# Three of the first layer's last four modulation chunks on VectorE, beside the input projection

## The chip, the cores and the metric

The kernel runs on one core of a Trainium2 chip. The metric is the device time of one execution in microseconds. A run of the program is timed as a whole; one execution is also profiled, and the profile gives the start and the duration of every instruction on every engine. In what follows the engines are called as the profile calls them: PE is TensorE (matmuls; PEld its weight loads), DVE is VectorE, ACT is ScalarE, POOL is GpSimd, and SP issues most DMAs.

## The reference

One inference step of a two-layer backbone, on 512 latent tokens and 128 context tokens of width 1024. What the change touches is the modulation, six vectors per layer and condition (shift, scale and gate of the mixer, then of the FFN):

```python
def modulation(cvec, w_mod, b_mod):
    m = jax.nn.silu(cvec) @ w_mod + b_mod
    return jnp.split(m[:, None, :], 6, axis=-1)

def run_trunk(x, cvec, p, past):
    ...
    for i in range(DEPTH):
        j = i // 2
        sh1, sc1, g1, sh2, sc2, g2 = modulation(cvec, p['w_mod'][i], p['b_mod'][i])
        h = rmsnorm(x, p['norm_mix'][i]) * (1.0 + sc1) + sh1
        if i % 2 == 0:
            ...
            mix, s_fin = even_mixer(h, p, j, s0)
        ...
        x = x + g1 * (mix @ p['w_out'][i])
        h = rmsnorm(x, p['norm_ffn'][i]) * (1.0 + sc2) + sh2
        x = x + g2 * conv_ffn(h, p['ffn_w_up'][i], p['ffn_conv_w'][i], p['ffn_conv_b'][i], p['ffn_w_down'][i])
```

There are two conditions: the vector c for the latent tokens and the constant c_ctx for the context tokens. A weight `w_mod[i]` is 1024 x 6144. The first layer's mixer (`even_mixer`) projects h to 3600 columns, runs four heads of a gated DeltaNet in both directions over chunks of tokens, and an implicit long convolution of order two (Hyena) on the other 512 columns.

## The kernel before, in words

Activations lie transposed, 128 features by 642 columns (512 latent tokens, a gap of two, 128 context tokens). A product with a weight is made of three matmuls with operands split in a high and a low part (lines 310 to 312); for that every weight tile `wr` is copied to `wwh` by ACT (line 304) and the rest taken to `wwl` by DVE (line 305).

Modulations come in chunks of 1024 columns, so six per layer, numbered as in the reference: 0 and 1 are needed before the first layer's projection, 2 (g1) by its output projection, 3 and 4 (shift and scale) by its FFN's norm, 5 (g2) at the end of its FFN. They are computed in one of two ways:

- `mod_chunk` on PE: eight steps over the 1024 rows. Each loads a 128 x 1024 piece of `w_mod` into a buffer `wr` and issues four matmuls with the two conditions as stationary operand (32 columns wide, four strips of the array) into one PSUM bank `modps`. `mod_finish` then copies the bank to SBUF (`mev`, ACT), transposes it twice on PE (`modt`) and adds the bias on DVE.
- `mod_rows` on DVE: the two conditions are loaded as rows spread over all partitions (`crow`) and put through SiLU on ACT; the weight comes transposed in pieces `mraw`; each piece of 128 x 512 is multiplied with the row of each condition and summed along the row by one instruction (line 257, output `mjunk`, sums in `mpart`). A chunk has 8 x 2 pieces and two conditions, so 32 such instructions, and two small additions at its end. All of layer 1's chunks are done in this way.

Chunks 0 and 1 of layer 0 run on PE in the prologue, among the filters of the Hyena part (`filters`). Then the input projection starts: `heads_in` and `hyena_in` call `unit_T`, a projection unit of 128 columns (a weight load, the split, 48 matmuls; its matmul results are called `mm`, the convolved result `cv`). `fills` yields, in this order, the second half of the heads, all Hyena units and the gates (`dn_gate`, `zT`); after these it sets `ready[0]`, and then comes the Hyena transform (`hyena_order`: matmuls `fx`, `iv`, `ivp`, with `rab`, `yab`, `hy` on the other engines). `with_mods` wraps this generator and puts a step of `fill_mods`, layer 0's chunks 2 to 5 by `mod_chunk`, behind each of its yields once `ready[0]` is set. The two together are the filling that `pull` takes from, one unit of cost for each yield of the DeltaNet rounds. A round runs two `dn_intra` side by side (bank `F`, tile `at`, decay `a`, first `dq` and `dx`, then six levels of `Q` - `Y`, `YT` - `dz`, `dx`, then `R`, `ZR`), and behind them the chain over chunks (`kS`, `vn`, `dS`, `qS`, `o`, with `dt`, `S`, `osum` on DVE). `outputs` normalises and gates finished chunks (`os`, `ok`, `ft`, `fs`).

This code gives each instruction a place and a priority; a scheduling layer then fixes the order on every engine before the run. At run time each engine takes its instructions in that order and waits for semaphores. So an engine's order is known from the built program, and what stands behind a waiting instruction waits too.

## Time and profile before

| | |
|---|---|
| runs shown (3) | 1879.08, 1882.99, 1884.51 us; median 1882.99 |
| profiled execution | 1880.43 us, of which the span from first to last instruction is 1878.7 |
| mean granted TensorE clock | 0.98 |
| PE busy | 1788.3 us, 95% |
| DVE busy | 1374.1 us, 73% |
| ACT busy | 848.1 us, 45% |
| POOL busy | 311.4 us, 17% |
| memory traffic | 215.61 MB read, 16.54 MB written |

The prologue lasts until about 81 us, when the first `mm` starts. The first round starts near 183 us; projection and rounds stand side by side until about 450 us; Hyena transforms, modulation steps and the last rounds until about 630 us, where layer 0's output projection starts. Busy shares are averages over stages with different limits. In the rows of the profile, "x" counts instructions, a bracket at the end of a row gives the idle time of that engine ahead of it and what ended it, and a row "A <- B: t, n, m" of the waits means that A waited t us in all for B, n times, m us at longest.

### The profile page before, as it was taken

Reading aid. Unit: us, or ns where it says so; the run is one execution under the profiler, and the core shown is the slowest. Engines: PE = TensorE matmul, PEld = TensorE weight load, DVE = VectorE, ACT = ScalarE, POOL = GpSimd, SP = SyncE. Lnnn points to the kernel's source line nnn. Section 1 sums busy time; section 2 is a strip of 40 time slices with the busy share of each in tenths; the row PEclk is TensorE's granted clock in tenths of the full one; section 3 lists DMA queues with packets and bytes.
Section 4 is the critical chain, followed back from the end, with each engine's and each line's share of the span. In section 5 each row is a group of like instructions: output and inputs, shape, how many; then the busy total and the mean of one; then the engine's idle time right before and its main releaser. Section 6 shows DMA issues by size and latency. Waiting matters only on the chain.

```text
span 1878.7 us, 31471 instructions
## 1 busy us (share of the span) xinstructions
PE 1788.3 (95%) x12052; PEld 1665.0 (89%) x12052; DVE 1374.1 (73%) x2896; ACT 848.1 (45%) x1678; POOL 311.4 (17%) x349
## 2 busy tenths in 40 slices
PE   5899999999888899999999999999999999999997
PEld 1578999998667899999999998977799999999997
DVE  5755666667887989886887888976778874774874
ACT  3555443433232436633634635445526651552653
POOL 2323442324544210000000003200000000000001
PEclk9899999999989999999999999999999999999999
DMA  8332112224544641555556563411242552552631
GB/s 292 128 104 77 36 57 74 67 72 138 176 168 139 234 141 53 143 186 141 138 183 168 130 217 138 140 53 40 91 180 62 146 152 57 146 139 74 160 90 57
DMA packets 86066, 234.20 MB, mean 125 GB/s; under 512 B 9080, under 2 KB 20728, under 8 KB 85786
## 3 DMA queue, kind: packets, MB, share of 16 engines
q1 hardware_dynamic: 66112, 192.45, 30.9%
q0 software_dynamic: 5760, 20.97, 6.7%
q10 hardware_dynamic: 14042, 18.76, 2.9%
q8 instruction: 95, 1.56, 0.3%
q14 instruction: 57, 0.47, 0.1%
HBM read 215.61 MB, written 16.54 MB: 124 GB/s over the span
## 4 chain that ended last, share of the span: by engine, by line
PE 72%; DVE 13%; ACT 3%; POOL 3%; issue 2%; DMA 2%; POOLq 0%; DVEq 0%; ACTq 0%
PE mm L310 10%; PE mm L312 10%; PE mm L311 10%; PE bx L310 4%; PE bx L311 4%; PE bx L312 4%; PE bv L312 2%; PE bv L310 2%; PE bv L311 2%; PE tr L1009 2%; PE fx L1395 1%; PE YT L1176 1%; PE Y L1174 1%; PE Q L1168 1%; PE o L1872 1%
## 5 line engine op out<-in xcount | busy, mean ns | idle before, releaser
L579 ACT CAST cwh<-wr 128x512 fp32r<-128x512 f32 x200 | 119.6, 621 | 144.8 <-PE bx L311 45.9
L304 ACT CAST wwh<-wr 128x1024 fp32r<-128x1024 f32 (+1 forms) x100 | 101.3, 1013 | 175.8 <-PE mm L311 133.9
L580 DVE TENSOR_TENSOR cwl<-wr,cwh 128x512 fp32r<-128x512 f32 x200 | 133.8, 686 | 36.2 <-ACT cwh L579 36.0
L305 DVE TENSOR_TENSOR wwl<-wr,wwh 128x1024 fp32r<-128x1024 f32 (+1 forms) x100 | 122.2, 1223 | 39.4 <-ACT wwh L304 38.6
L310 PE MATMUL mm<-h0h,wwh 128*128 128x384 f32 (+2 forms) x448 | 148.5, 331 | 0.5 <-DVE d L850 0.2
L446 DVE SCALAR_TENSOR_TENSOR x<-mm,mod,x 128x128 f32<-128x128 f32 (+3 forms) x192 | 77.5, 436 | 95.0 <-PE mm L312 94.8
L311 PE MATMUL mm<-h0l,wwh 128*128 128x384 f32 (+2 forms) x448 | 140.1, 313 | 0.0
L591 POOL DMA_DIRECT2D t<-in_w_up x40 | 34.5, 864 | 633.4 <-DMA t<-in_w_up 150.0
L312 PE MATMUL mm<-h0h,wwl 128*128 128x384 f32 (+2 forms) x448 | 139.3, 311 | 0.0
L257 DVE SCALAR_TENSOR_TENSOR mjunk<-mraw,crow 128x512 f32<-128x512 f32 x192 | 125.3, 685 | 1.9 <-DMA mraw<-in_w_modT 1.4
L310 PE MATMUL od<-owh,h2h 128*128 128x256 f32 x320 | 97.0, 305 | 0.1
L679 DVE SCALAR_TENSOR_TENSOR cv<-ab,par,cv 128x641 f32<-128x641 f32 x88 | 77.7, 883 | 25.2 <-ACT cv L677 24.4
L312 PE MATMUL od<-owh,h2l 128*128 128x256 f32 x320 | 91.5, 289 | 2.1 <-DVE h2l L430 1.3
L311 PE MATMUL od<-owl,h2h 128*128 128x256 f32 x320 | 90.5, 284 | 0.0
L310 PEld LDWEIGHTS mm<-h0h,wwh 128*128 128x128 f32 x448 | 85.3, 190 | 3.7 <-issue 1.8
L1139 POOL TENSOR_TENSOR am<-a,msk 128x512 fp32r<-128x512 f32 x60 | 73.0, 1225 | 92.4 <-PE Q L1168 81.2
L311 PEld LDWEIGHTS mm<-h0l,wwh 128*128 128x128 f32 x448 | 84.8, 189 | 0.5 <-issue 0.2
L312 PEld LDWEIGHTS mm<-h0h,wwl 128*128 128x128 f32 x448 | 84.5, 189 | 0.1
L726 DVE SCALAR_TENSOR_TENSOR cv<-mm,par,cv 128x382 f32<-128x382 f32 (+2 forms) x96 | 52.1, 544 | 32.5 <-ACT cv L720 31.7
L579 ACT CAST cwh<-t 128x512 fp32r<-128x512 f32 x80 | 48.0, 622 | 47.5 <-PE bx L311 17.3
L437 ACT ACTIVATE sq<-x 128x320 f32<-128x320 f32 (+4 forms) x63 | 31.5, 501 | 78.7 <-DVE x L446 64.8
L310 PEld LDWEIGHTS od<-owh,h2h 128*128 128x128 f32 x320 | 60.4, 189 | 4.5 <-issue 4.2
(555 smaller groups left out, 6170.7 us busy)
## 6 DMA issues: line engine op xcount, KB each, us to landing
wr<-in_w_mod SPq DMA_DIRECT2D x48, 512.0 KB, 4.6
wr<-in_w_up SPq DMA_DIRECT2D x48, 512.0 KB, 4.2
mraw<-in_w_modT SPq DMA_DIRECT2D x40, 512.0 KB, 5.5
t<-in_w_up SPq DMA_DIRECT2D x80, 256.0 KB, 3.1
t<-in_w_up POOLq DMA_DIRECT2D x40, 512.0 KB, 5.5
wr<-in_w_in SPq DMA_DIRECT2D x28, 512.0 KB, 3.3
wr<-in_w_dn SPq DMA_DIRECT2D x32, 448.0 KB, 3.5
wr<-in_w_up SPq DMA_DIRECT2D x40, 256.0 KB, 3.7
```

Source lines behind the costliest of these rows:

```text
L257: nc.vector.scalar_tensor_tensor(out=junk, in0=w[:, c : c + 512], scalar=1.0, in1=rows[m][:, c0 + c : c0 + c + 512], op0=ALU.mult, op1=ALU ...
L304: nc.scalar.copy(hi[:, :K], src)
L305: nc.vector.tensor_tensor(out=lo[:, :K], in0=src, in1=hi[:, :K].bitcast(F32), op=ALU.subtract)
L310: nc.tensor.matmul(ps, l[0](k), r[0](k), start=start, stop=False, skip_group_check=more)
L311: nc.tensor.matmul(ps, l[0](k), r[1](k), start=False, stop=False, skip_group_check=more)
L312: nc.tensor.matmul(ps, l[1](k), r[0](k), start=False, stop=stop, skip_group_check=more)
L446: nc.vector.scalar_tensor_tensor(out=xt[:, a:b], in0=ps[:, a - c0 : b - c0], scalar=mcol(layer, ch, d, m), in1=xt[:, a:b], op0=ALU.mult, o ...
L579: nc.scalar.copy(hi, src)
L580: nc.vector.tensor_tensor(out=lo, in0=src, in1=hi.bitcast(F32), op=ALU.subtract)
L679: nc.vector.scalar_tensor_tensor(out=t[:, c0:c1], in0=ar[:, c0 + s_ : c1 + s_], scalar=w[i], in1=t[:, c0:c1], op0=ALU.mult, op1=ALU.add)
L726: nc.vector.scalar_tensor_tensor(out=t[:, c0:c1], in0=p[:, c0 + s_ - a : c1 + s_ - a], scalar=w[i], in1=t[:, c0:c1], op0=ALU.mult, op1=ALU ...
L1139: eng.tensor_tensor(out=v(out), in0=v(a32), in1=msk[:, lv, :, None, :].broadcast_to([P, 2, 2, P]), op=ALU.mult)
```

## The change

Chunks 2, 3 and 4 of layer 0 leave `fill_mods` and go to `mod_rows` on DVE, which now takes the layer as an argument. `with_mods` draws them before `ready[0]` is set: each yield of the projection with cost c adds 0.44 c to a debt, and pieces (cost 1.55 each) are issued until it is paid. The pieces use a pool of their own, `rowp` (two rows `crow`, three `mraw` of 128 x 512). Chunk 5 stays in `fill_mods`. `mev` moves from a buffer of its own to the shared temporary `fs`, and the host lays out the transposed weights for both layers.

```diff
--- before.py
+++ after.py
@@ -64,6 +64,9 @@
 
 LANES = ((0,), ((1,), (2,), (3,)), (4,), (5,))
 
+EARLY = (2, 3, 4)
+EARLY_RATE = 0.44
+
 
 PCOL = {}
 
@@ -219,7 +222,7 @@
         yield 0.45
 
     def mod_finish(layer, ch, ps):
-        ev = wpool.tile([P, 256], F32, tag="mev", name=nm("mev"), bufs=1)
+        ev = tmp.tile([P, NT], F32, tag="fs", name=nm("mev"))[:, :256]
         nc.scalar.copy(ev, ps[:, :256])
         yield
         pt = s_ps("modt")
@@ -236,7 +239,7 @@
 
     mpart = perm.tile([P, KD, 2, 2], F32, tag="mpart", name="mpart")
 
-    def mod_rows(chunks, row, raw, n):
+    def mod_rows(chunks, row, raw, n, layer=1):
 
 
 
@@ -249,7 +252,7 @@
             for d in range(KD):
                 for c0 in range(0, 1024, n):
                     w = raw()
-                    nc.sync.dma_start(w, A["w_modT"][ch, d][:, c0 : c0 + n])
+                    nc.sync.dma_start(w, A["w_modT"][layer, ch, d][:, c0 : c0 + n])
                     for c in range(0, n, 512):
 
                         junk = tmp.tile([P, NT], F32, tag="ft", name=nm("mjunk"))[:, :512]
@@ -259,10 +262,10 @@
                                 op0=ALU.mult, op1=ALU.mult, accum_out=mpart[:, d, m, (c0 + c) // 512 : (c0 + c) // 512 + 1],
                             )
                     if d == KD - 1 and c0 + n == 1024:
-                        to = mod[:, 1, 8 * ch : 8 * ch + 8, :]
+                        to = mod[:, layer, 8 * ch : 8 * ch + 8, :]
                         nc.vector.tensor_tensor(out=to, in0=mpart[:, :, :, 0], in1=mpart[:, :, :, 1], op=ALU.add)
                         nc.vector.tensor_tensor(
-                            out=to, in0=to, in1=pc("b_mod", 48 + 8 * ch, 8)[:, :, None].broadcast_to([P, 8, 2]), op=ALU.add
+                            out=to, in0=to, in1=pc("b_mod", 48 * layer + 8 * ch, 8)[:, :, None].broadcast_to([P, 8, 2]), op=ALU.add
                         )
                     yield 1.55 * n / 512
 
@@ -784,6 +787,7 @@
         return lambda i, n=1: (t[0][:, i : i + n, :] if i < 10 else t[1][:, i - 10 : i - 10 + n, :]).rearrange("p n q -> p (n q)")
 
     dnc = dn_stack.enter_context(tc.tile_pool(name="dnc", bufs=2))
+    rowp = dn_stack.enter_context(tc.tile_pool(name="rowp", bufs=2))
     filt_stack = dn_stack.enter_context(ExitStack())
     fp = filt_stack.enter_context(tc.tile_pool(name="filt", bufs=1))
 
@@ -1519,6 +1523,8 @@
         for hp in range(2):
             zTs[hp] = yield from dn_gate(hp)
         ready[0] = True
+        for _ in early:
+            yield 0.0
         for hf in range(2):
             hyena_load(hf)
             for o in range(2):
@@ -1527,13 +1533,21 @@
             later(hyena_out(hf, *mix.pair(2 + hf)))
             yield from outputs(heads[0])
 
-    fill_mods = mods([(0, ch) for ch in range(2, 6)], mm_ps)
+    fill_mods = mods([(0, ch) for ch in range(2, 6) if ch not in EARLY], mm_ps)
     ready = [False]
+    early = mod_rows(
+        EARLY, lambda: rowp.tile([P, 1024], F32, tag="crow", name=nm("crow")),
+        lambda: rowp.tile([P, 512], F32, tag="mraw", name=nm("mraw"), bufs=3), 512, 0,
+    )
+    owed = [0.0]
 
     def with_mods(gen):
         for c in gen:
             yield c
             step()
+            owed[0] += EARLY_RATE * c
+            while owed[0] > 0.0 and not ready[0]:
+                owed[0] -= next(early, 1e9)
             if ready[0]:
                 yield next(fill_mods, 0.0)
 
@@ -2132,7 +2146,7 @@
         put(name, np.tile(i[name].reshape(64, 1), (2, 1)))
     a["params"] = par
     a["w_mod"] = i["w_mod"][0]
-    a["w_modT"] = np.stack([i["w_mod"][1][:, 1024 * ch : 1024 * ch + 1024].T.reshape(KD, P, D) for ch in range(6)])
+    a["w_modT"] = np.stack([i["w_mod"][l].T.reshape(6, KD, P, D) for l in range(2)])
     a["c_rows"] = np.stack([i["c"][0], i["c_ctx"]], 0)
     w = i["ev_w_in"][0]
     col = lambda o, n=256: w[:, o : o + n]
```

What it does to the order, at three places. First DVE, near the end of the projection (about 404 to 412 us of the profile before). Before:

```order
L1263 SCALAR_TENSOR_TENSOR osum_1453<-qS_3999,eg,osum_1453 128x128 x4
L305 TENSOR_TENSOR wwl_4182<-wr_4179,wwh_4181 128x1024
L726 SCALAR_TENSOR_TENSOR cv_4051<-mm_4008,par,cv_4051 128x259
L726 SCALAR_TENSOR_TENSOR cv_4051<-mm_4008,par,cv_4051 128x258
L1273 TENSOR_TENSOR osum_1453<-o_4079,osum_1453 128x256 x2
L1178 TENSOR_TENSOR dz_4096<-Y_4086,dz_3969 128x512
L1179 TENSOR_TENSOR dx_4097<-YT_4087,dx_3970 128x512
L1178 TENSOR_TENSOR dz_4122<-Y_4112,dz_3995 128x512
L1179 TENSOR_TENSOR dx_4123<-YT_4113,dx_3996 128x512
```

and now, from behind the same first `osum` to the same first `dz` (line numbers of the changed kernel are three to four higher):

```order
L260 SCALAR_TENSOR_TENSOR mjunk_4335,mpart<-mraw_4333,crow_757 128x512
L260 SCALAR_TENSOR_TENSOR mjunk_4397,mpart<-mraw_4395,crow_756 128x512
L260 SCALAR_TENSOR_TENSOR mjunk_4397,mpart<-mraw_4395,crow_757 128x512
L260 SCALAR_TENSOR_TENSOR mjunk_4462,mpart<-mraw_4460,crow_756 128x512
L260 SCALAR_TENSOR_TENSOR mjunk_4462,mpart<-mraw_4460,crow_757 128x512
L308 TENSOR_TENSOR wwl_4425<-wr_4422,wwh_4424 128x1024
L729 SCALAR_TENSOR_TENSOR cv_4284<-mm_4241,par,cv_4284 128x259
L260 SCALAR_TENSOR_TENSOR mjunk_4534,mpart<-mraw_4532,crow_756 128x512
L729 SCALAR_TENSOR_TENSOR cv_4284<-mm_4241,par,cv_4284 128x258
L1277 TENSOR_TENSOR osum_1517<-o_4312,osum_1517 128x256 x2
L260 SCALAR_TENSOR_TENSOR mjunk_4534,mpart<-mraw_4532,crow_757 128x512
L1182 TENSOR_TENSOR dz_4329<-Y_4319,dz_4197 128x512
```

Five `mjunk` now stand ahead of `wwl` (the low half of a weight unit), and one each between the two `cv` and ahead of `dz`.

Second DVE again, while the filters still run beside the first heads (about 144 to 151 us; `e`, `d` are filter taps, `ye` their butterflies). Before:

```order
L726 SCALAR_TENSOR_TENSOR cv_1204<-mm_1098,par,cv_1204 128x382
L726 SCALAR_TENSOR_TENSOR cv_1204<-mm_1098,par,cv_1204 128x383
L850 TENSOR_TENSOR e_1122<-f_199_1180,dec_852 128x256
L850 TENSOR_TENSOR d_1123<-f_199_1180,dec_852 128x256
L305 TENSOR_TENSOR wwl_1362<-wr_1359,wwh_1361 128x1024
L726 SCALAR_TENSOR_TENSOR cv_1204<-mm_1167,par,cv_1204 128x259
L769 TENSOR_TENSOR ye_1240<-e_1122 128x512
```

and now:

```order
L859 SCALAR_TENSOR_TENSOR d_1162<-d_1162,hyb 1x256
L260 SCALAR_TENSOR_TENSOR mjunk_1361,mpart<-mraw_1359,crow_756 128x512
L729 SCALAR_TENSOR_TENSOR cv_1253<-mm_1137,par,cv_1253 128x382
L260 SCALAR_TENSOR_TENSOR mjunk_1361,mpart<-mraw_1359,crow_757 128x512
L729 SCALAR_TENSOR_TENSOR cv_1253<-mm_1137,par,cv_1253 128x383
L260 SCALAR_TENSOR_TENSOR mjunk_1407,mpart<-mraw_1405,crow_756 128x512
L854 TENSOR_TENSOR e_1161<-f_215_1224,dec_871 128x256
L854 TENSOR_TENSOR d_1162<-f_215_1224,dec_871 128x256
L260 SCALAR_TENSOR_TENSOR mjunk_1407,mpart<-mraw_1405,crow_757 128x512
L308 TENSOR_TENSOR wwl_1421<-wr_1418,wwh_1420 128x1024
L729 SCALAR_TENSOR_TENSOR cv_1253<-mm_1211,par,cv_1253 128x259
L772 TENSOR_TENSOR ye_1289<-e_1161 128x512
```

Four `mjunk` stand between these and ahead of `wwl`; in all twelve `mjunk` now lie between the last butterfly before this place and `ye`.

Third PE in a round beside the Hyena transform (about 515 to 523 us; `tr`, `KQ`, `Q`, `Y`, `YT` belong to the round). Before:

```order
L1156 MATMUL KQ_5164<-T_2064,khT_1812 128x128 x4
L1168 MATMUL Q_5172<-dz_5120,am_5170 128x128 x4
L1395 MATMUL fx_5181<-hy_5046,dft_f_4559 128x256
L1168 MATMUL Q_5196<-dz_5150,am_5194 128x128 x4
L212 MATMUL modps_4957<-wr_5203,cs 32x256 x4
L1395 MATMUL fx_5224<-hy_5047,dft_f_4559 128x256 x4
L1174 MATMUL Y_5235<-dq_5177,dx_5111 128x128 x4
L1176 MATMUL YT_5236<-dx_5111,dq_5177 128x128 x4
L1174 MATMUL Y_5249<-dq_5201,dx_5141 128x128 x4
L1176 MATMUL YT_5250<-dx_5141,dq_5201 128x128 x4
L212 MATMUL modps_4957<-wr_5263,cs 32x256 x4
L1397 MATMUL fx_5273<-u_916_4850,dft_f_4559 128x256 x2
```

and now:

```order
L1160 MATMUL KQ_5408<-T_2170,khT_1903 128x128 x4
L1172 MATMUL Q_5416<-dz_5363,am_5414 128x128 x4
L1172 MATMUL Q_5438<-dz_5387,am_5436 128x128 x4
L1178 MATMUL Y_5470<-dq_5421,dx_5354 128x128 x4
L1180 MATMUL YT_5471<-dx_5354,dq_5421 128x128 x4
L1178 MATMUL Y_5484<-dq_5443,dx_5378 128x128 x4
L1180 MATMUL YT_5485<-dx_5378,dq_5443 128x128 x4
L1440 MATMUL iv_5498<-dft_i_4818,yab_5293 128x256 x4
L1172 MATMUL Q_5511<-dz_5480,am_5509 128x128 x4
L1440 MATMUL iv_5518<-dft_i_4817,yab_5292 128x256 x4
L1172 MATMUL Q_5530<-dz_5494,am_5528 128x128 x4
```

The `modps` steps are gone, and the transform's `iv` stand where its `fx` stood: the transform runs further ahead of the round.

## The prediction

> **What bounds the kernel now.** I read the page's busy shares first, then the busy time of each engine by stage (one row per stretch; the columns are the stretch, its length, then each engine's busy us, the granted clock, the DMA share), and then the chain of waits for the one stage whose engines all have idle time.
>
> ```profile
> PE 1788.3 (95%) x12052; PEld 1665.0 (89%) x12052; DVE 1374.1 (73%) x2896; ACT 848.1 (45%) x1678; POOL 311.4 (17%) x349
> ```
> ```profile
> core 0: us, PE busy (x) PEld busy (x) DVE busy (x) ACT busy (x) POOL busy (x), PEclk, DMA share, GB/s
> 95.00:200.00 105.00, 95.89 (x574) 84.27 (x574) 61.03 (x138) 54.59 (x103) 30.37 (x33) 1.00 0.25 83
> 200.00:450.00 250.00, 247.02 (x1877) 243.77 (x1877) 162.40 (x295) 105.08 (x175) 83.70 (x91) 1.00 0.21 69
> 487.00:640.00 153.00, 133.52 (x879) 108.34 (x879) 126.86 (x259) 44.56 (x79) 67.86 (x73) 0.91 0.47 156
> 700.00:1000.00 300.00, 295.90 (x1978) 293.38 (x1978) 242.09 (x486) 145.36 (x267) 13.21 (x22) 0.99 0.50 142
> ```
>
> TensorE is the bound over the kernel as a whole: 95%. From 200 to 450 us, where the input projection fills the gaps of the DeltaNet rounds, it is idle for 3 us of 250 while VectorE is idle for 88. From 487 to 640 us, where the projection is used up and the Hyena transforms stand beside the rounds, neither is full: TensorE 133.5 of 153 at a granted clock of 0.91, VectorE 126.9. The change takes work off the second stretch and puts other work into the first two.
>
> What the removed steps cost: in the rows below, the modulation matmuls (line 212), and the chain that ended last over 486 to 640 us.
>
> ```profile
> L212 PE MATMUL modps<-wr,cs x384: 379/403/636, 6.9 to 593.4; 128*32 128x256 f32 x192
> 482.61 0.57 PE modps L212 x8
> by line: PE fx L1395 13.8%; issue 7.2%; PE iv L1430 6.5%; PE modps L212 3.9%; POOL ok L194 2.5%; PE tr L1009 2.3%; DVE ft L1328 2.2%; POOL rab L1404 2.0%; DVE u L1461 2.0%; DVE hy L769 1.9%; PE R L1185 1.9%; DVE ok L1326 1.9%; PE YT L1176 1
> PE Q L1168 <- DVE dz L1178: 4.8, 3, 3.0
> PE tr L1009 <- DVE dx L1147: 4.1, 1, 4.1
> PE tr L1009 <- DVE ft L1328: 3.6, 3, 1.3
> ```
>
> One step of a chunk (four packed matmuls, eight records) moves the chain on by 0.57 us; a chunk has eight steps. The page counts six chunks (384 records): two in the prologue, four here. The first of the four is over by 487 us, and in the changed program one chunk stays and takes exactly that place. So 3 x 8 = 24 steps go, all from 487 to 640 us.
>
> **The change part by part.** The profiled execution took 1880.43 us (span 1878.7); the runs shown have a median of 1882.99, which is 2.6 above it. I sum against 1880.4 and add the 2.6 at the end. A difference under about 0.3% (5.6 us) is not told from none here.
>
> 1. *Matmuls removed.* 24 x 0.57 = 13.7 us of TensorE, and six transposes with about 1 us: 14.7 at most. But modps holds only 3.9% of the chain's 154 us, 6.0 us; the other steps fill time in which TensorE would wait for dz, dx or ft from VectorE, as the three waits above show. Ends: 0 (VectorE, 83% busy, is late everywhere) and 14.7. I take 6.0, since the chain's row is the nearest.
>
> 2. *Multiply-accumulates added.* Each chunk is 8 x 2 x 2 = 32, so 96. The same instruction already runs later, beside layer 1's work:
>
> ```profile
> L257 DVE SCALAR_TENSOR_TENSOR mjunk<-mraw,crow x192: 671/685/694, 644.4 to 1404.5; 128x512 f32<-128x512 f32 x192
> L257 DVE DVE_READ_ACCUMULATOR mjunk<-mraw,crow x192: 74/82/89, 645.0 to 1405.1; 128x1 f32 x192
> ```
>
> 96 x (0.685 + 0.082) = 73.6 us of VectorE. The new order puts 24 of them before the first round (about 183 us) and 72 from there to about 410 us. VectorE from 200 to 450 us becomes 162.4 + 72 x 0.767 = 218 of 250, 87%. From 700 to 1000 us it is 81% busy and TensorE loses only 1.4%; from 487 to 640 us it is 83% busy and TensorE loses 13%. These are the two ends for the 250 us stretch: 0 to 29 us. I take a value near the first, because in the new order TensorE's rows there are the same as before, with twelve projection matmuls between most hand-offs, and because I followed the worst place by hand: seven new instructions stand between two osum groups and the next dz.
>
> ```profile
> 403.73 1.12 DVE L1263 SCALAR_TENSOR_TENSOR osum<-qS,eg,osum 128x128 f32<-128x128 f32 x4
> 405.99 1.23 DVE L305 TENSOR_TENSOR wwl<-wr,wwh 128x1024 fp32r<-128x1024 f32 x1 [1.14 <-ACT wwh L304]
> 408.46 0.76 DVE L1273 TENSOR_TENSOR osum<-o,osum 128x256 f32<-128x256 f32 x2 [0.33 <-PE o L1269]
> 409.13 0.68 DVE L1178 TENSOR_TENSOR dz<-Y,dz 128x512 fp32r<-128x512 f32 x1
> 411.86 0.69 DVE L1178 TENSOR_TENSOR dz<-Y,dz 128x512 fp32r<-128x512 f32 x1 [1.45 <-PE Y L1174]
> 413.59 1.95 PE L1185 MATMUL R<-dz,a 128*128 128x128 f32 x16
> ```
>
> 7 x 0.767 = 5.4 us, less the idle 1.14 and 0.33: the first dz is 4.0 us late and ends at 413.8, the second, whose gap of 1.45 is used up too, at 415.1 where it was 412.5. R starts at 413.59 and its second half 0.9 us later; it is held for 0.6 us. Lateness of 4 us costs TensorE 0.6. The other clusters are of one to four instructions, in front of idle times of 1 to 2 us. I charge 1 us for the rounds.
>
> 3. *The same before the first round, beside the filters.* Here TensorE does wait for VectorE, since the filters' butterflies have nothing else beside them:
>
> ```profile
> 146.67 0.43 DVE L850 TENSOR_TENSOR e<-f,dec 128x256 f32<-128x256 f32 x1 [1.13 <-PE f L843]
> 149.27 1.23 DVE L305 TENSOR_TENSOR wwl<-wr,wwh 128x1024 fp32r<-128x1024 f32 x1 [1.85 <-ACT wwh L304]
> 151.13 1.21 DVE L769 TENSOR_TENSOR ye<-e 128x512 f32<-128x512 f32 x1 [0.23 <-POOL e L848]
> PE hsp L867 <- DVE ye L772: 0.9, 2, 0.5
> ```
>
> The new order has twelve of them, 9.2 us, between the butterflies that end near 126 us and this place. Carried row by row through VectorE's idle times between them (each takes back only what was late before it), the wwl is still some 2.4 us late; ye has 0.23 in hand, and everything to the matmuls on ye follows. Ends: 0 (the later idle time takes it back) and 24 x 0.767 = 18. I take 2.
>
> 4. *Rows of c and their SiLU on ScalarE.* Two activations, and four more table loads (the program has 27 where it had 23), between about 70 and 115 us:
>
> ```profile
> L247 ACT ACTIVATE crow<-crow 128x1024 f32<-128x1024 f32 x12 | 12.7, 1063 | 3.5 <-DMA crow<-in_c_rows 3.5
> L979 ACT ACT_TABLE_LOAD  x1: 1283/1283/1283, 100.6 to 100.6; - x1
> PE gc L991 <- ACT spfs L979: 2.1, 1, 2.1
> ```
>
> 2 x 1.06 + 4 x 1.28 = 7.2 us. ScalarE is 52% busy from 95 to 200 us, yet TensorE waits 2.1 us for it at gc. Ends: 0 and 7.2; I take 1.5, below the wait that is there, since the new order puts more projection ahead of gc.
>
> 5. *One gated output moved.* os, ok and ft of the first finished pair of chunks, at 391 to 401 us before, now come after the projection, in the stretch that lost the matmuls.
>
> ```profile
> 390.89 0.68 DVE L1319 TENSOR_REDUCE os<-fs 128x4 f32<-128x512 f32 x1
> 393.28 1.13 DVE L1326 TENSOR_TENSOR ok<-ok,rq 128x4 f32<-128x4 f32 x1 [1.12 <-POOL ok L194]
> 400.87 0.69 DVE L1328 TENSOR_TENSOR ft<-osum,ok 128x512 f32<-128x512 f32 x1 [2.16 <-DMA hx<-cv]
> ```
>
> With the small ones between them, some 3 us of VectorE move into a stretch where VectorE is part of the chain: 0 to 3, I take 1.5.
>
> 6. *Contention with GpSimd.* The 192 existing instructions run where GpSimd does almost nothing (13 us of 300); the new ones run where it is busy for 84 of 250. An instruction that reads two SBUF tensors is longer there, and GpSimd's own are longest in such company:
>
> ```profile
> L305 DVE TENSOR_TENSOR wwl<-wr,wwh 128x1024 fp32r<-128x1024 f32 x26 | 36.2, 1391 | 21.6 <-ACT wwh L304 21.6
> L305 DVE TENSOR_TENSOR wwl<-wr,wwh 128x1024 fp32r<-128x1024 f32 x8 | 9.8, 1223 | 2.8 <-ACT wwh L304 2.6
> L1139 DVE TENSOR_TENSOR dq<-a,msk 128x512 fp32r<-128x512 f32 x8 | 8.4, 1074 | 0.0
> L1139 POOL TENSOR_TENSOR am<-a,msk x60: 1149/1167/2145, 185.3 to 568.5; 128x512 fp32r<-128x512 f32 x60
> ```
>
> The same wwl is 1391 ns on average from 100 to 450 us and 1223 from 700 to 1000, 14% more. At 14% the 96 grow by 9 us of VectorE time, at dq's 1074 ns by 37. Most of it lies in idle time; on the path I charge 1 of the 9. The Trainium skill ("GPSIMD Engine Reference", Key points) says that GpSimd shares its SBUF interfaces with VectorE and that VectorE instructions with two SBUF inputs contend there; it speaks against this change, and the rows agree. By that rule, with every new instruction at dq's length, the case is the first slower rival below.
>
> 7. *At no charge.* The 48 loads of 256 KB that SP now issues between the loads of w_in go where DMA is 21% busy; if one waits for its buffer, the w_in load behind it waits too, but three weight buffers stand for units some 12 us long. One VectorE pair instead of a transpose and an add at the end of a chunk is under 1 us. The rest of the program, from 640 us on, does the same work.
>
> Sum: -6.0 + 1 + 2 + 1.5 + 1.5 + 1 = +1.0 on 1880.4, so 1881.4 for such an execution and, with the 2.6, 1884 us.
>
> **The rivals.**
>
> *Hidden entirely (faster).* VectorE's 88 idle us swallow all of it, terms 2 to 6 are 0, and more than the chain's share of the steps comes back because Hyena's matmuls move up into the steps' places. The end is 1880.4 - 14.7 + 2.6 = 1868; half way between it and the sum without charges (1877) is 1873. For it: the 700 to 1000 us stretch with VectorE at 81%. Against: three waits for VectorE that no removed matmul shortens.
>
> *VectorE late in the rounds (slower).* The new order has nine clusters of three to five in the rounds. If contention stretches them to dq's length, three are 3.5 us where idle times of 1 to 2 stand before a dz; past that the rest falls on TensorE, 1.5 us for each of nine: 13 more, 1897. It decides from the point where a dz comes more than about 4 us late. For it: am at 2145 ns at worst. Against: term 2's place, where 4 us cost 0.6.
>
> *A colder clock (slower).* The removed steps also kept TensorE going in the gaps. After a gap of 4.1 us the same step takes nearly twice as long:
>
> ```profile
> 508.74 1.09 PE L1009 MATMUL tr<-ident,dx 128*128 128x128 f32 x4 [4.14 <-DVE dx L1147]
> 509.76 1.07 PE L212 MATMUL modps<-wr,cs 128*32 128x256 f32 x6
> 517.62 0.64 PE L212 MATMUL modps<-wr,cs 128*32 128x256 f32 x8
> ```
>
> If the granted clock from 487 us on goes from 0.91 to 0.85, some 120 us of matmuls take 7 to 9 us more: 1891. The Trainium skill ("TensorE: Matmul & The Clock Gate", Part 1) says that the clock halves after an idle window of about 3.4 us; the row agrees with a gap of that size. Against: the gaps lie at the start of the rounds and are there already.
>
> **How the numbers follow.** Forecast (within 0.3%, its own range 1878 to 1889) 0.44; hidden 0.26; VectorE late 0.22; clock 0.08. Faster 0.26, same 0.44, slower 0.30. The range takes in the middle of the faster rival and of the slower ones, 1872 to 1897, and leaves out the full 14.7 and two charges at their ends together.
>
> **What would show it.** Right: line 212's records fall from 384 to 192, 96 more mjunk between 90 and 415 us with a mean of 0.70 to 0.85 us, the last R before the Hyena stage within 4 us of its old time, 487 to 640 us shorter by 3 to 6. Wrong towards faster: no wait of TensorE for VectorE grows before 450 us and the last stretch loses over 9. Wrong towards slower: TensorE's waits for dz, dx or the filters' ye grow by over 8 us in sum, or the clock after 487 us falls below 0.87.

## The result, and the profile after

The changed kernel takes 1900.25 us (median of four runs, 1896.15 to 1905.84) where the kernel before takes 1881.53 (four runs, 1879.08 to 1884.51): a ratio of 1.0104, with a 95% interval of 1.0076 to 1.0131. It is 1% slower; the forecast was no change, and the range ended at 1897. The profiled execution took 1905.84 us (span 1904.1) and is the slowest of the four, 25.4 us of span above the profiled one of before, so its stages show where such time goes but overstate the median by some 6 us.

The busy line of the page of after, and the busy time by stage over the stretches that the prediction used:

```profile
PE 1789.1 (94%) x11854; PEld 1672.2 (88%) x11854; DVE 1437.3 (75%) x3091; ACT 855.3 (45%) x1681; POOL 321.5 (17%) x349
```
```profile
core 0: us, PE busy (x) PEld busy (x) DVE busy (x) ACT busy (x) POOL busy (x), PEclk, DMA share, GB/s
95.00:200.00 105.00, 95.38 (x552) 84.26 (x545) 71.10 (x183) 57.23 (x106) 30.12 (x31) 0.97 0.38 125
200.00:450.00 250.00, 242.72 (x1817) 237.72 (x1815) 210.37 (x432) 105.28 (x170) 85.71 (x87) 0.99 0.29 91
487.00:640.00 153.00, 121.83 (x692) 106.09 (x691) 126.45 (x239) 41.76 (x75) 76.22 (x78) 0.85 0.23 74
700.00:1000.00 300.00, 294.68 (x1950) 290.90 (x1950) 239.21 (x469) 149.63 (x274) 13.46 (x21) 0.98 0.50 138
```

198 of TensorE's records are gone, and yet it is busy for 0.8 us longer than before. In the last column but two the granted clock is below before's in every row; from 487 to 640 us it is 0.85 where it was 0.91. What the change was to do, it did: the modulation records are half as many, and 96 products run between 98 and 424 us (the matmuls of line 215, then the products on the tile mjunk from 90 to 455 us; ns at least, median and most, first and last start):

```profile
L215 PE MATMUL modps<-wr,cs x192: 379/634/637, 6.7 to 496.3; 128*32 128x256 f32 x192
```
```profile
L260 DVE SCALAR_TENSOR_TENSOR mjunk<-mraw,crow x96: 616/686/1678, 97.8 to 424.1; 128x512 f32<-128x512 f32 x96
```

Five landmarks on TensorE split the 25.4 us (the first matmul of the projection, the first G, the last R ahead of the Hyena stage, the first matmul on mix, the first FFN matmul pu). First before, where the R at 413.59 stands in the prediction, then after:

```profile
80.97 0.49 PE L310 MATMUL mm<-h0h,wwh 128*128 128x384 f32 x1
...
182.84 0.61 PE L1128 MATMUL G<-khT 128*128 128x128 f32 x4
...
630.79 0.39 PE L310 MATMUL mm<-mixh,wwh 128*128 128x320 f32 x1
...
698.82 0.84 PE L310 MATMUL pu<-a11h,wwh 128*128 128x320 f32 x2 [0.18 <-ACT a11h L527]
```
```profile
83.78 0.44 PE L313 MATMUL mm<-h0h,wwh 128*128 128x384 f32 x1
...
189.49 0.72 PE L1132 MATMUL G<-khT 128*128 128x128 f32 x5
...
426.28 0.83 PE L1189 MATMUL R<-dz,a 128*128 128x128 f32 x6
...
641.28 0.40 PE L313 MATMUL mm<-mixh,wwh 128*128 128x322 f32 x1
...
714.29 0.63 PE L313 MATMUL pu<-a11h,wwh 128*128 128x320 f32 x1
```

- to the first projection matmul +2.8, from there to the first G +3.8 (forecast for both: +3.5);
- first G to the last R +6.0 (forecast +2);
- last R to the first pu +2.8: -2.2 to the first matmul on mix, +5.0 behind it (forecast -4.5);
- first pu to the end +9.9 (forecast 0).

Single executions scatter at these marks. The first G comes at 182.8, 185.1 and 186.4 us in three kernels that share before's code up to there (before, e11, e14 below) and at 188.5 to 190.8 in five that share after's (after, e7, e8, e12, e13), so of the 6.7 us up to the first G about 5 belong to the change. The time from there to the last R is steadier: 230.5 to 230.8 us in the six with before's work there (before, e1, e5, e6, e11, e14), 236.8 to 242.2 in the eight with all 96 products and their loads (after, e3, e7, e8, e12, e13, e17, e18).

The stretch that lost 13.7 us of matmuls did not shrink. TensorE's waits there, from 499 to 641 us (what is waited for: us in total, times, longest):

```profile
PE Q L1172 <- DVE dz L1182: 11.7, 3, 5.0
PE fx L1399 <- DVE hy L774: 4.5, 2, 4.0
PE R L1189 <- DVE dz L1182: 4.3, 1, 4.3
PE tr L1013 <- DVE ft L1332: 2.7, 1, 2.7
PE Y L1178 <- DVE at L1166: 2.4, 1, 2.4
PE tr L1013 <- DVE dx L1151: 2.1, 1, 2.1
```

Before, Q on dz was 4.8 and R on dz did not appear. TensorE now waits in a stretch where it ran modulation steps, and behind each wait of 2.4 us or more matmuls run at half speed (behind one of 2.1 us they do not). One such place in after, the timeline first, then the busy time and the clock of the 3.4 us with the gap and of the 6.8 us behind:

```profile
533.31 0.66 PE L1178 MATMUL Y<-dq,dx 128*128 128x128 f32 x4 [0.23 <-ACT dq L1174]
...
536.86 1.08 PE L1178 MATMUL Y<-dq,dx 128*128 128x128 f32 x4 [2.44 <-DVE at L1166]
```
```profile
533.00:536.40 3.40, 1.19 (x9) 0.97 (x8) 3.38 (x5) 0.75 (x2) 2.17 (x2) 0.98 0.26 83
536.40:543.20 6.80, 6.34 (x21) 5.65 (x22) 3.12 (x6) 0.63 (x2) 0.18 (x1) 0.51 0.01 2
```

The same four matmuls take 0.66 us ahead of the gap and 1.08 behind it. This gap of 2.4 us is paid for again with up to 3.4 us (6.8 us at half speed). The Trainium skill ("TensorE: Matmul & The Clock Gate", Part 1) gives a free-running window of about 3.4 us, cold after an idle one, warm after a busy one. The traces agree on the length (apart from the last one, the half-speed stretches of before and after last 3.4, 6.8, 13.7 or 17.1 us, steps of 3.4), but the window ahead of the drop was not idle: TensorE was busy for 1.19 of its 3.4 us.

### The profile page after: what moved, and what is told of

The parts are those of the page before. It is cut to its first block, busy times and chain, and to the rows that moved or that the text cites. A ratio compares the mean times of both kernels' runs of the same rounds, so it can differ in the third digit from the quotient of the medians.

```text
span 1904.1 us, 31384 instructions
## 1 busy us (share of the span) xinstructions
PE 1789.1 (94%) x11854; PEld 1672.2 (88%) x11854; DVE 1437.3 (75%) x3091; ACT 855.3 (45%) x1681; POOL 321.5 (17%) x349
## 4 chain that ended last, share of the span: by engine, by line
PE 70%; DVE 14%; DMA 5%; POOL 4%; issue 3%; ACT 3%; POOLq 0%; DVEq 0%; ACTq 0%; SPq 0%
PE mm L313 10%; PE mm L314 9%; PE mm L315 9%; PE bx L313 4%; PE bx L315 4%; PE bx L314 4%; PE bv L315 2%; PE bv L313 2%; PE bv L314 2%; PE tr L1013 2%; DMA wr<-in_w_mod 2%; DMA wr<-in_w_up 2%; PE fx L1399 1%; PE od L315 1%; PE o L1886 1%
## 5 line engine op out<-in xcount | busy, mean ns | idle before, releaser
L260 DVE SCALAR_TENSOR_TENSOR mjunk<-mraw,crow 128x512 f32<-128x512 f32 x288 | 199.2, 714 | 11.8 <-DMA mraw<-in_w_modT 5.3
L1143 POOL TENSOR_TENSOR am<-a,msk 128x512 fp32r<-128x512 f32 x60 | 80.2, 1344 | 96.0 <-PE Q L1172 88.4
L582 ACT CAST cwh<-t 128x512 fp32r<-128x512 f32 x80 | 47.9, 622 | 43.6 <-PE bx L314 15.9
```

The source lines that it names most:

```text
L260: nc.vector.scalar_tensor_tensor(out=junk, in0=w[:, c : c + 512], scalar=1.0, in1=rows[m][:, c0 + c : c0 + c + 512], op0=ALU.mult, op1=ALU ...
L582: nc.scalar.copy(hi, src)
L1143: eng.tensor_tensor(out=v(out), in0=v(a32), in1=msk[:, lv, :, None, :].broadcast_to([P, 2, 2, P]), op=ALU.mult)
```

## Experiments

Every run comes with its mean granted clock, so each kernel's time can be split. "Clock loss" is (1 - mean clock) x median time, taken against the runs of before that were measured beside it; it bounds from above what half speed costs, since TensorE is not busy all the while. "Rest" is the other part of the difference of the medians. (For after, the clock of before is that of one execution, 0.980.)

| kernel | ratio to before, 95% | mean clock | clock loss, us | rest, us |
|---|---|---|---|---|
| after | 1.0104, 1.0076 to 1.0131 | 0.9740 | +11.8 | +6.9 |
| e1 place only | 1.0033, 1.0020 to 1.0047 | 0.9811 | +5.4 | +0.9 |
| e2 remove only | 1.0052, 1.0035 to 1.0069 | 0.9770 | +13.2 | -1.7 |
| e3 add only | 1.0064, 1.0043 to 1.0086 | 0.9807 | +6.3 | +6.5 |
| e4 rounds only | 1.0105, 1.0083 to 1.0128 | 0.9750 | +17.2 | +3.9 |
| e5 fs only | 1.0025, 1.0016 to 1.0034 | 0.9823 | +2.0 | +1.3 |
| e6 remove, paced | 1.0050, 1.0037 to 1.0064 | 0.9768 | +12.4 | -4.0 |
| e7 after, paced | 1.0101, 1.0088 to 1.0115 | 0.9745 | +17.1 | +1.3 |
| e8 after, warm | 1.0074, 1.0062 to 1.0086 | 0.9780 | +10.3 | +2.8 |
| e9 loads and SiLU | 1.0086, 1.0064 to 1.0108 | 0.9780 | +9.8 | +5.8 |
| e10 products only | 1.0052, 1.0033 to 1.0072 | 0.9811 | +3.7 | +4.8 |
| e11 before, warm | 1.0024, 1.0004 to 1.0044 | 0.9812 | +3.6 | +0.7 |
| e12 after, warm at waits | 1.0115, 1.0092 to 1.0139 | 0.9762 | +13.3 | +8.3 |
| e13 after, warm twice | 1.0119, 1.0102 to 1.0137 | 0.9820 | +3.9 | +18.7 |
| e14 before, warm steps | 1.0059, 1.0042 to 1.0076 | 0.9838 | +0.2 | +10.5 |
| e15 loads only | 1.0091, 1.0076 to 1.0106 | 0.9785 | +10.4 | +7.0 |
| e16 SiLU only | 1.0021, 1.0009 to 1.0033 | 0.9812 | +5.1 | -0.7 |
| e17 after, own mev | 1.0118, 1.0098 to 1.0137 | 0.9744 | +16.8 | +6.8 |
| e18 own mev, warm | 1.0086, 1.0073 to 1.0099 | 0.9790 | +7.9 | +8.0 |

### The parts of the change, each by itself (e1 to e5)

**e1**, all of the change but the work:

```
-    fill_mods = mods([(0, ch) for ch in range(2, 6) if ch not in EARLY], mm_ps)
+    fill_mods = mods([(0, ch) for ch in range(2, 6)], mm_ps)
-    early = mod_rows(EARLY, ...)
+    (the early buffers reserved, unused)  early = iter(())
```

> The work of the kernel before, in its order (all four chunks on the matmuls, no early rows), with everything else of the change: the transposed weights of both layers in one tensor, the early buffers reserved but unused, the pools behind them shifted, mev taken from the tag fs. Theory A (the work moved is what costs): 1879 to 1885 us, as before; w_out, FFN and attention stages from 640 us take what they took. Theory B (the loss of about 10 us after 699 us and of 2.8 us ahead of the first projection matmul comes from where the data lie, in DRAM or in SBUF): 1891 to 1897, with the first projection matmul at 83 to 84 us where it was 81.0.

1.0033, 6.3 us over the median of before measured beside it: more than theory A's nothing, half of what theory B asked, though no work was moved. The time from the first pu to the end (1178.3 us; before 1179.9) speaks against B; the first projection matmul, 5.3 us late, says that something happens in the prologue.

**e5** asks what, with one line changed in before:

```
-        ev = wpool.tile([P, 256], F32, tag="mev", name=nm("mev"), bufs=1)
+        ev = tmp.tile([P, NT], F32, tag="fs", name=nm("mev"))[:, :256]
```

> The kernel before with one line changed: mev is taken from the tag fs instead of its own buffer; data layout and pools as before. The order of the instructions is then the one of e1 (30 rows of PE up to about 110 us stand elsewhere). Theory A (what e1 loses, 1.0033, is the order of the prologue): ratio 1.002 to 1.005, the first projection matmul at 84 to 86 us. Rival B (what e1 loses comes from where the data lie): ratio within 0.999 to 1.001.

1.0025: the shared buffer alone gives most of it, theory A, and the first projection matmul comes at 86.2 us. Since mev and the squares of the norm now take turns in fs, the prologue is put in another order, and modulation steps stand ahead of the filters' matmuls. TensorE's wait for their weights from 0 to 60 us, before and e5:

```profile
PE modps L212 <- DMA wr<-in_w_mod: 14.2, 8, 7.8
```
```profile
PE modps L212 <- DMA wr<-in_w_mod: 20.1, 10, 8.1
```

**e2**, the removal without the added work:

```
-    early = mod_rows(EARLY, ...)
+    def blank():
+        nc.vector.memset(mod[:, 0, 16:40, :], 0.5)
+        yield 1.0
+    early = blank()
```

> As after, with the early rows left out: chunks 2 to 4 of layer 0 are filled with a constant, so 24 steps of matmuls are gone and nothing is added. Theory A: 1867 to 1877 us; 6 to 14.7 us less than before, all between 487 and 645 us, and the start of each round as before within 2 us. Rival C (colder clock: the steps kept TensorE going in its gaps): 1880 to 1888, since TensorE's clock in the slices from 500 to 625 us falls below 0.9 and the steps' time is not given back. Theory B: as A or C with 10 us more after 640 us.

1.0052, and 1.0033 with the matmuls in place (e1). With 13.7 us of TensorE work taken away and nothing added, one run of ten (1880.1; the others up to 1892.3) lies below e1's median of 1881.1. The rest is 2.6 us better than e1's, the clock loss 7.8 worse. That fits rival C's account and not A's. (The profiled run is the fastest of the ten, so its stages are not read here.)

**e3**, the addition without the removal:

```
-    fill_mods = mods([(0, ch) for ch in range(2, 6) if ch not in EARLY], mm_ps)
+    fill_mods = mods([(0, ch) for ch in range(2, 6)], mm_ps)
     early = mod_rows(..., 512, 0, <a spare tile for the sums>)
```

> As after, with all four chunks kept on the matmuls too: the 96 multiply-accumulates, their 48 loads, the rows of c and their SiLU are added, their sums go to a spare tile. Theory A: the last R before the Hyena stage is 12 to 13 us late as in after (426 us where it was 413.6), and since no matmul is gone the end is 1891 to 1897 us or more. Rival C (the clock is what the removal costs): this kernel loses 12 us by 426 us and gives part of it back, 1885 to 1892, below after's 1900. Theory B: 1900 to 1907.

1.0064: a kernel that does all of before's work and all of after's is nearer to before than after is. Its last R is at 425.0 us, nearly as late as in after, so the loss up to there is that of the added work and the prologue. The matmuls that stay are then worth some 0.4%, with intervals that overlap.

**e4**, no product before the first round:

```
+    nc.gpsimd.memset(mod[:, 0, 16:24, :], 0.5)
     early = mod_rows(
-        EARLY, ...
+        LATE, ...                       # chunks 3 and 4
-            while owed[0] > 0.0 and not ready[0]:
+            while begun and owed[0] > 0.0 and not ready[0]:
```

> As after, but the early rows begin with the first round of the DeltaNet instead of beside the input projection and the filters, and one of the three chunks (chunk 2) is filled with a constant instead: 64 multiply-accumulates, all in the rounds, at the same rate; the rows of c are read and their SiLU taken there too. Theory A in its form that what stands before the first round costs 4 us (terms 3 and 4 of the sum) and the rounds 6: the first G of the first round is back at 184 to 186 us (before 182.8, after 189.5), the last R at 420 to 423, the end at 1894 to 1897. If the part before the first round is hidden by later idle time: the last R at 425 to 427 and 1899 to 1901.

Both forms missed. The products started at 181.7 us, and still the first G came at 191.8, later than in after (189.5), and the ratio is after's with 64 products in place of 96. The 24 products beside the filters are not what makes the first round late. The run does not clear the rest of the early work: the loads of mraw were still issued from 57.7 us on, and the SiLU of the rows, which was expected in the rounds, still ran at 99 to 107 us.

### Why the removal costs: order or clock (e6 to e8)

**e6** and **e7** put an empty step of the same weight at each removed one, in e2 and in after, so that the fill is pulled as before:

```
+    def holes():
+        for ch in EARLY:
+            ps = mm_ps("modps")
+            for k in range(KD):
+                yield 0.45
+    fill_mods = chain(holes(), mods([(0, 5)], mm_ps))
```

> e2 (24 steps removed, nothing added), with an empty step of the same 0.45 in the fill at each place of a removed one, so that what is pulled beside each round is as before and Hyena no longer runs ahead of the chains. Theory A (the removal costs through the order it causes: the chain's tail is left uncovered at w_out): ratio 0.997 to 1.002 against e2's 1.0052, and first Hyena output to first FFN matmul 66 to 68 us where e2 had 73.6. Rival C (it costs through the clock: the matmuls kept TensorE warm in its gaps): ratio 1.004 to 1.008, and a mean clock of 0.975 to 0.978 as in e2.

> After, with the same empty steps: the change with the order of before from 487 us on. Theory A: 1.004 to 1.007, 5 to 10 us below after. Rival C: 1.009 to 1.012, as after.

1.0050 and 1.0101, as e2 and after. The order from 487 us on is before's again, the gated output is back in its place, and nothing is gained: theory A falls, rival C stays. From 487 to 634 us, e5 and then e6:

```profile
487.00:634.00 147.00, 129.52 (x875) 104.62 (x874) 124.14 (x250) 41.65 (x76) 74.19 (x77) 0.93 0.45 146
```
```profile
487.00:634.00 147.00, 122.61 (x728) 105.22 (x728) 124.38 (x241) 41.30 (x73) 72.27 (x76) 0.88 0.27 86
```

The same stretch, the same VectorE work, 7 us less of TensorE and a clock of 0.88 for 0.93; the waits of Q for dz go from 4.8 to 8.7 us:

```profile
PE Q L1168 <- DVE dz L1178: 4.8, 3, 3.1
```
```profile
PE Q L1172 <- DVE dz L1182: 8.7, 3, 4.7
```

**e8** fills the same places with matmuls whose operands are in SBUF:

```
+                for j in range(4):
+                    nc.tensor.matmul(ps[32 * j : 32 * j + 32, :256], cs[:, k, :], cmat..., ...)
                 yield 0.45
```

> After, with the removed matmuls put back in number and place but on operands that are in SBUF anyway (their sums are dropped): TensorE does what it did before, VectorE does the early rows, and the 24 loads of 512 KB stay away. Theory A and rival C both: 1.005 to 1.008 as e3 (1.0064), since order and warmth are back, and the mean clock at 0.979 to 0.983. If the loads of the removed steps were what delayed other transfers: 1.000 to 1.004. If neither order nor warmth matter: 1.010.

1.0074 against e7's 1.0101, the intervals just apart: 24 useless steps make the kernel 0.27% faster. The loads are still absent, so it is not they. The clock is 0.978, a step towards the expected 0.979 to 0.983. From 498 to 642 us, e7 and then e8:

```profile
498.00:642.00 144.00, 120.28 (x720) 103.01 (x719) 120.40 (x234) 39.69 (x71) 72.24 (x73) 0.89 0.25 81
```
```profile
498.00:642.00 144.00, 127.03 (x855) 102.81 (x855) 119.83 (x238) 39.75 (x72) 74.31 (x76) 0.92 0.26 83
```

The pair repeats with mev in its own buffer (e17 and e18, below): 1.0118 without, 1.0086 with.

Where the removal's cost lies is less clear than its sign. The profiles of the four pairs (with matmuls there, without) differ as follows; "half speed" is half of the time that the clock stood at 0.5, "rest" the remainder, in us:

| pair | first G to first pu | half speed | rest | first pu to the end | half speed | by the medians |
|---|---|---|---|---|---|---|
| e1, e2 | +3.8 | +10.2 | -6.4 | +0.3 | -5.8 | +5.2 |
| e5, e6 | +0.9 | +8.5 | -7.7 | +8.9 | +3.1 | +5.1 |
| e8, e7 | +1.0 | +5.1 | -4.1 | +6.3 | +0.1 | +5.2 |
| e18, e17 | +1.1 | +10.5 | -9.4 | +1.1 | -2.8 | +7.7 |

In the part that held the steps their time does come back, 4 to 9 us of it, and half speed takes all of that and 1 to 4 us more. This is why nothing is gained. That it comes out 5 to 8 us worse by the medians is not shown there: in the two pairs whose profiles are about 9 us apart, most of the difference lies behind the first pu, in work that did not change, and half speed explains at most a third of it there. These are single executions, and those of e2 and e17 were faster than their kernels' medians; e6 also has e1's places of the data, which e5 has not.

### Is there a dose, and does the place matter (e11 to e14)

**e11** puts twelve resident matmuls ahead of the two transposes of dx in before's last round, **e12** four ahead of every transpose of dx, Q and R of after's:

```
+    def warm_ps(s, n=3):                # e12: n=1
+        ps = d_ps(s)
+        for j in range(4 * n if ready[0] else 0):
+            (one resident matmul into ps)
+        return ps
-        ps = tr([X[:, b].bitcast(F32) for b in BLK], d_ps)
+        ps = tr([X[:, b].bitcast(F32) for b in BLK], warm_ps)
```

> The kernel before with twelve matmuls on resident data (1.7 us) ahead of each of the two transposes of dx in the last round, where TensorE waited 4.1 us for dx and then ran at half clock for 6.8 us; their sums are dropped. Clock theory (a gap costs its length and then up to 3.4 us more): the slices from 508 us on stay at 1.00, one such stretch less, ratio 0.997 to 1.000, faster although TensorE does more. If warmth at one place only moves the cold stretch: 1.000 to 1.002.

> After with four matmuls on resident data (0.57 us) ahead of every transpose of dx, Q and R of the round that follows the projection, the places where after's TensorE waits longest (Q 11.7, R 4.3, dx 2.1 us). Clock theory: as good as e8, which put them at the removed steps' places: 1.005 to 1.008, mean clock 0.977 to 0.981. If only the old places help: 1.010 or more, since the added matmuls stand on the chain.

1.0024, which is not faster, and 1.0115, no better than after. In e11 the mean clock did not rise (0.9812; before beside it 0.9830). In e12 it rises a little (0.9762; after 0.9740, e7 0.9745), but the rest rises as well; that matmuls directly ahead of a waiting one stand on the chain would explain it and is not shown by itself.

**e13** doubles e8's matmuls, **e14** adds four to each modulation step of before's last stretch:

```
-                for j in range(4):
+                for j in (0, 1, 2, 3) * 2:
```

> e8 with twice the matmuls on resident data at each of the 24 places (eight in place of four, 1.1 us of TensorE a step). e7, with none, stood at 1.0101, e8, with four, at 1.0074. Clock theory with a dose: 1.004 to 1.007, and the mean clock above e8's 0.978. If four were enough and the rest only fills: 1.007 to 1.009. If the added matmuls stand on the chain: 1.010 or more.

> The kernel before with four more matmuls on resident data behind each of the 32 modulation steps in the stretch from 487 us on, 18 us of TensorE in all, whose sums are dropped. Clock theory with a dose: 0.994 to 0.999, a kernel that is faster for doing more. If the steps of before are already enough: 1.000 to 1.004. If the added matmuls stand on the chain: 1.006 or more.

1.0119 and 1.0059. In after the clock obeys: with none, four and eight matmuls a step the loss is 17.1, 10.3 and 3.9 us. The time does not: the rest goes 1.3, 2.8, 18.7 us. At 0.57 us for four, 24 steps are 13.7 us of TensorE; the first four add 1.5 us of that to the rest, the next four 15.9, as if they stood on the chain in full. In before (e14) not even the clock obeys: its loss is level with before's. So the dose theory is right for the clock of after and wrong for the time, and before's steps were already the useful amount.

### Which part of the added work costs (e9, e10, e15, e16)

All four are e3 with part of the early work left out: e9 has one tiny multiplication in place of the two products of each load, e10 takes the products from rows filled by GpSimd, with no early load and no SiLU, e15 is e9 without the rows of c and their SiLU, e16 is e9 without the loads.

```
e9   +  nc.vector.tensor_tensor(out=dst[:, 0, :], in0=w[:, 0:2], in1=rows[0][:, 0:2], op=ALU.mult)
e10  -  w = raw(); nc.sync.dma_start(w, ...)      +  w = rows[1][:, c0 : c0 + n]
```

> e3 (all chunks on the matmuls, early work added) without the products: the rows of c, their SiLU on ScalarE with its table loads and the 48 loads of 256 KB are there, VectorE does one tiny multiplication for each load in place of two products. e1, which has none of it, stood at 1.0033, e3, which has all, at 1.0064. If VectorE's products cost the 0.3%: 1.003 to 1.004. If ScalarE's activations or the transfers do: 1.006 to 1.007.

> e3 with the 96 products on rows that stand in SBUF: no early load, no SiLU on ScalarE, the same 74 us of VectorE. If VectorE's products cost the 0.3% between e1 and e3: 1.006 to 1.007, the last R before the Hyena stage at 424 to 426 us. If ScalarE or the transfers do: 1.003 to 1.004.

> e9 without the rows of c and their SiLU: the 48 early loads of 256 KB, one tiny VectorE instruction for each, rows filled by GpSimd. e1, without loads, 1.0033; e9 1.0086. If the transfers make the difference: 1.006 to 1.009. If ScalarE's SiLU does: 1.003 to 1.004.

> e9 without the 48 loads: the rows of c are read and go through SiLU on ScalarE with four more table loads, and the tiny VectorE instructions work on them. If ScalarE's SiLU makes the difference between e1 and e9: 1.006 to 1.009, with the first gc at 116 to 121 us (e1 109.7, e9 120.6). If the transfers do: 1.003 to 1.004.

1.0086, 1.0052, 1.0091, 1.0021. Both expectations of e10 missed: its 1.0052 lies between them, with the last R at 429.4 in a profiled run that was the slowest of its nine. SiLU on ScalarE with its table loads costs nothing over e1, though the first gc came at 115.5 us, almost as late as was expected if it did. The products cost 0.2% over e1, with intervals that overlap. The loads look dearest, but e9 and e15 do not stand for after: without the products to wait for, SP sends the 48 loads by 186 and 178 us, while with them they reach to 417. The loads of mraw in e15, then in e3 (issue time, first and last):

```profile
L258 SPq DMA_DIRECT2D mraw<-in_w_modT x48: 327/328/1172, 52.1 to 178.0; - x48
```
```profile
L255 SPq DMA_DIRECT2D mraw<-in_w_modT x48: 327/328/650, 53.8 to 416.8; - x48
```

Bunched beside the prologue and the filters they cost 0.5 to 0.6% more than e1; spread, with the products, 0.3% (e3). How much of that 0.3% is loads and how much products stays open.

### Do the costs add (e17, e18)

mev has its own buffer again, in after (e17) and in e8 (e18):

```
+        ev = wpool.tile([P, 256], F32, tag="mev", name=nm("mev"), bufs=1)
-        lambda: rowp.tile([P, 512], F32, tag="mraw", name=nm("mraw"), bufs=3), 512, 0,
+        lambda: rowp.tile([P, 512], F32, tag="mraw", name=nm("mraw"), bufs=2), 512, 0,
```

> After with mev in a buffer of its own again (1 KB, taken from the early loads, which have two buffers of 256 KB in place of three). The order up to the first early load is before's again. If the parts add (mev in fs 1.0025 to 1.0033, removal 0.2%, early work 0.3 to 0.5%): 1.0065 to 1.008, the first projection matmul back at 81 to 82 us. If the loss ahead of the first round comes from the early work whatever the prologue does: 1.009 to 1.011.

> e8 (after with 24 steps of matmuls on resident data) and e17's mev together: the two costs of the change that can be undone without giving up what it moves. If the parts add: 1.0035 to 1.0055, what is left being the early work beside the filters and the rounds. A version of the change that beats the kernel before would need less than 0.999, which no theory gives.

1.0118 and 1.0086: they do not add. The first projection matmul, expected back at 81 to 82 us, came at 85.1 and 85.3. TensorE's wait for the modulation weights is back near before's there (14.8 us, before 14.2), but a wait of 4.5 us for ScalarE's hst, ahead of the projection, has come in. The shared buffer costs 0.25% in a kernel without early work, and giving it up wins nothing in one with it (the early loads also had a buffer less). No version beat the kernel before, and the best of those that keep the change is e8.

### What stays open: the time after the first pu

After's 9.9 us there are in work that did not change. In the thirteen profiled experiments that have the steps, or other matmuls for them, it takes 1176.8 to 1180.6 us from the first pu to the end; in those without, 1178.7 (e2), 1179.1 (e17), 1183.1 (e4), 1185.4 (e7), 1186.2 (e6), and 1189.8 in after. One place is the end of layer 0's FFN, where VectorE waits for parts of w_up. From 1013 to 1114 us of after, and the 101 us of e5 that answer to them (999 to 1100):

```profile
DVE wr L602 <- DMA t<-in_w_up: 8.1, 1, 8.1
...
DVE wr L602 <- DMA wr<-in_w_up: 4.4, 3, 2.1
```
```profile
DVE wr L599 <- DMA wr<-in_w_up: 0.3, 1, 0.3
```

TensorE gets some 3 us of it there. Another is a transpose (tr) between 1216 and 1326 us that waits for ScalarE's oy: 3.8 us in e5 and 4.0 in e8, 5.3 in e7, 5.6 in e6 and after, 5.7 in e4. Half speed is not it: of after's 9.9 us it is 1.6. Why transfers land later in four of six such kernels was not found: SP's order of loads is the same in e7 and e8, and e13 has such waits too, without the loss. These are single executions.

## Why the prediction was wrong, point by point

- **Term 1, matmuls removed, -6.0: this step failed, by its sign.** It took the steps' share of the chain as time that comes back. Measured four times, with matmuls in place against without (e1 and e2, e5 and e6, e8 and e7, e18 and e17), the removal costs 0.2 to 0.3%, 5 to 8 us by the medians. In the profiles the rest does improve between the first G and the first pu, by 4.1 to 9.4 us, so the 6.0 was a fair size for it; the 5.1 to 10.5 us of half speed that come with it were not in the term. That a matmul is on the chain that ended last does not say that the chain is shorter without it: behind it stood waits for VectorE of nearly the same end. What the removal costs beyond this cancelling is not placed; part of it shows behind the first pu, and its cause stays open.
- **The colder clock**, a rival at a chance of 0.08, is what cancelled the gain. Its sign came as written (0.85, below 0.87), and its price, 7 to 9 us, is near the measured 5.1 to 10.5; what was wrong was to weigh it as a case apart from term 1, and to argue against it that the gaps were there already. They were there and got longer: Q on dz from 4.8 to 11.7 us. It does not explain the whole loss: its 1891 us lie 9 below the measured median.
- **Not in the sum: mev in the tag fs.** The diff showed that line, and no term priced it. Alone it costs 0.25% (e5), 3 to 5 us, in the prologue, ahead of all moved work. After's first projection matmul is 2.8 us late, 14 us before the first product runs, but it is no earlier with mev in its own buffer (e17), so that the shared buffer causes this delay in after is not shown.
- **Terms 3 and 4, +3.5 before the first round:** 6.7 in the profile, about 5 by the kernels that share the code. The split does not hold: without products there the loss stays (e4, which kept the early loads and the SiLU in front), and SiLU alone costs nothing (e16: first KQ at 194.5, before 194.9). Which part of the early work makes the first round late stays open.
- **Terms 2 and 6, +2 in the rounds: mis-sized**, 6 to 11 (236.8 to 242.2 us from the first G to the last R, before 230.8). In after, TensorE is idle for 7.3 us of 250 where it was 3.0, and from the first G to 450 us up to 3.4 us go to half speed, where before's clock was full. Two things were read wrongly. The 73.6 us counted the overlap of product and read-out twice, since a read-out starts while its product still runs: the 192 products of before occupy VectorE for 126.1 us, 63 for 96. And contention, 9 us of VectorE with 1 on the path, did come at nearly that size. The 96 products take 770 ns on average where before's take 685, 8 us in all. Of the 32 that run beside a GpSimd instruction, 14 take 0.93 to 1.68 us; the 64 with none beside them average 683 ns. The row of the 96 (busy us, then mean ns), then one of the 14 with its neighbour on GpSimd (start, us):

```profile
L260 DVE SCALAR_TENSOR_TENSOR mjunk<-mraw,crow 128x512 f32<-128x512 f32 x96 | 73.8, 770 | 6.2 <-issue 2.7 <-ACT T L1501 1.9 <-PE tr L1013 0.6
```
```profile
292.61 1.53 DVE L260 SCALAR_TENSOR_TENSOR mjunk<-mraw,crow 128x512 f32<-128x512 f32 x1
```
```profile
292.32 1.28 POOL L1143 TENSOR_TENSOR am<-a,msk 128x512 fp32r<-128x512 f32 x1 [8.53 <-PE Q L1172]
```

  The Trainium skill ("GPSIMD Engine Reference", Key points) has VectorE instructions with two SBUF inputs contend with GpSimd; the trace agrees. The rival built on it, VectorE late in the rounds, priced 13 us; about half of that or more came, and how much of it is contention no run separates.
- **Term 5, the moved output, +1.5:** nothing. e6 and e7, which have it back in its place, are as slow as e2 and after.
- **Term 7, no charge: failed twice.** Early loads are not free (e15, e9, where they crowd), and "the rest does the same work" was true of the work and not of its time, +9.9 in the profile, open above.
- **What would show it:** the halved records, the 96 products and their length came true; the last R within 4 us did not (+12.7), nor a stretch shorter by 3 to 6. Both signs of "wrong towards slower" came: in the stretch from 487 us on the waits for dz and dx grew from 8.9 to 18.1 us, and the clock fell to 0.85.
- **The chances:** 0.30 for slower was too little, since three costs of one sign (prologue, early work, half speed) stood against one gain that was itself in doubt.

## What to carry to other kernels

A TensorE step that runs while another engine is late costs almost nothing, and its removal can win nothing or lose: ask what TensorE will do in its place, and if the answer is "wait", look at the granted clock behind the waits that exist already. Price every line of a diff, also the one that only shares a buffer, because it can reorder a stretch that nothing else touches. And before moving work off an engine, run the removal alone: here it lost 0.2% (e2 against e1), so no cheaper way to do the moved work would have helped.

## What the runs showed of the hardware

- A gap need not be complete or long to halve the clock: 2.44 us without a matmul, in a window of 3.4 us that was busy for 1.19, were followed by 6.8 us at 0.51.
- VectorE products with two SBUF inputs took up to 1.68 us beside a GpSimd instruction, against 0.70 at most for the 64 with none beside them.
- The clock differs between runs of one program: before's mean lay between 0.979 and 0.989 in the 21 runs beside e1, and their times between 1871.1 and 1881.3 us, the fastest at the highest clock.
- Matmuls that compute nothing can pay for themselves, once: 24 steps of four gave 0.27%, twice as many took it back (1.0119).
